# A bias table's way to its skewed form, and the place of one set of transposes, in a two-layer hybrid encoder

## The chip, the cores and the metric

The kernel runs on one core of one Trainium2 chip. Its time is the device time of one execution in microseconds (us). The core has five engines that run side by side and meet at semaphores: TensorE (PE: matmuls, and PEld, its weight loads), VectorE (DVE), ScalarE (ACT), GpSimd (POOL) and SyncE (SP), which here only issues DMA transfers. Transfers can be issued from SyncE's queue or from GpSimd's; both are carried out by the same 16 DMA engines.

## The reference, cut to what matters

Two layers work on 256 tokens of width 2048. Each layer reads RMSNorm(x) through one input projection, whose columns feed three mixers (gated linear attention, dilated windows with a relative bias, cross attention to a memory of 256 tokens), adds the output projection, then adds a squared-ReLU MLP of width 8192. All of it is float32.

```python
for l in range(DEPTH):
    h = rms_norm(x, norm_mix[l])
    proj = jnp.einsum('bsd,dk->bsk', h, w_in[l])
    (g_q, g_k, g_v, g_r, lr_f, lr_b, d_q, d_k, d_v, m_q) = split_columns(proj, IN_SPLITS)
    gla_out = gla_mixer(g_q, g_k, g_v, g_r, lr_f, lr_b, ...)
    dil_out = dilated_mixer(d_q, d_k, d_v, rel_bias, dil_norm[l])   # bias = rel_table[t5_bucket(j - i)]
    mem_out = memory_mixer(m_q, mem, mem_norm[l], w_mem_kv[l], mem_out_norm[l])
    mixed = jnp.concatenate([gla_out, dil_out, mem_out], axis=-1)
    x = x + jnp.einsum('bsk,kd->bsd', mixed, w_out[l])
    h = rms_norm(x, norm_mlp[l])
    u = jnp.square(jax.nn.relu(jnp.einsum('bsd,df->bsf', h, w_up[l])))
    x = x + jnp.einsum('bsf,fd->bsd', u, w_down[l])
```

## The kernel before

**Products.** Every float32 product is made of three matmuls on rounded halves: a weight quad (four blocks of 128 x 512, 1 MB, tile `raw`, three buffers) is loaded by `load_quad` (L189), ScalarE rounds it to `wh` (L203), VectorE makes the remainder `wl` (L204), each in two halves, and TensorE runs 24 matmuls per quad against the high and low halves of the activations (L221 to L223). `linear` does this for the four quads of one projection of 512 columns; `col(i)` is `linear` on the i-th such block of the input projection. `evac` (L231, ScalarE) scales a finished projection into a slot of a ring of 22 buffers that most of the kernel's middle tiles share.

**Order around the change.** The first layer starts with the memory: the keys' projection, then `bias_products`, then the values' projection, then `spread_bias`, then `col(9)` (the memory query mq), `col(0)` (the GLA query gq), `col(1)` (the GLA key gk), the memory attention, the gates, `col(2)` and `col(3)` (the GLA values), the GLA weights, and on to `col(6)`. The second layer runs in the same order without the bias. The activations of layer 0 come in transposed (`xT`, four pieces loaded by `split_loaded`, L173, the halves being x00h to x03h and x00l to x03l); `x` itself is loaded by GpSimd's queue (L569) once the squares of the memory have been taken from the same tile.

**The bias table.** `bias_products` makes, with one small matmul, `rows`: for each of 4 heads one row of 512 values by distance, in four partitions of on-chip memory. `spread_bias` (L259) writes each row 128 times into `scr`, a DRAM scratch of [4 heads, 128, 576]. `late_constants` (L275) reads `scr` back with a row step of 575, so that each partition gets its row shifted by one, as `bt` [128, 4, 384]. The dilated attention adds `bt` to its scores (L294).

**Transposes.** The operands of the attentions and of the GLA weights have to lie transposed. VectorE turns them in 16 blocks of 32 x 256 each (L108). These are generators in a work list, `turning`: `linear` takes one step (`turn(1)`) behind each quad's `wl`, and `issue_after` keeps the step's instructions behind that `wl`. km takes six steps (0, 4, 4, 4, 4 blocks, then the halves), mq four (0, 8, 8, then the halves), gq and gk six each (0, 4, 4, 4, 4, then the name is set). `turn()` without a number empties the list at once; `while "gkT" not in heads: turn(1)` ahead of the GLA weights takes the steps still missing, both without `issue_after`. The order of each engine's instructions is set when the kernel is built, by a planner with a model of the time; on the chip each engine works its list in order.

The lines and names that the steps below use: L173, L189, L203, L204, L221 to L223, L259, L275, L294, L569; tiles `raw`, `wh`, `wl`, `rows`, `scr`, `bt`, `gqT`, `gkT`, `gl` (the last tile of the gates, L391), `m_att`.

Of the kernel before, what the change touches and what calls it, by code (L numbers as in the profile page):

```python
# [11 lines left out]
F32 = mybir.dt.float32  # L12
# [8 lines left out]
P = 128  # L21
# [6 lines left out]
H = 4  # L28
# [9 lines left out]
NW = 512  # L38
# [4 lines left out]
def trunk_kernel(ctx: ExitStack, tc: tile.TileContext, a: dict):  # L43
    nc = tc.nc
# [7 lines left out]
    dram = ctx.enter_context(tc.tile_pool(name="scratch", bufs=1, space=DRAM))  # L52

    def slot(shape, name, dt=F32):
        return ring.tile([P] + shape, dt, tag="r", name=name)
# [15 lines left out]
    pending, turning = deque(), deque()  # L71

    def flush(n=None):
        for _ in range(len(pending) if n is None else min(n, len(pending))):
            pending.popleft()()
# [26 lines left out]
    def turn_blocks(o, v):  # L102

        src = v.rearrange("p t (b c) -> p t b c", b=4)
        dst = o.rearrange("p b (t s) -> p t b s", t=NT)
        for f in range(0, P, 32):
            for s in range(0, P, 32):
                yield nc.vector.transpose(  # L108
                    dst[f:f + 32, :, :, s:s + 32], src[s:s + 32, :, :, f:f + 32]
                )  # L110

    def paced(turns, steps):
        for n in steps:
            for _ in range(n):
                next(turns)
            yield
# [39 lines left out]
    def heads_turned(v, name, heads):  # L156

        o = slot([H, S], name)
        yield from paced(turn_blocks(o, v), (0, 4, 4, 4, 4))
        heads[name] = o  # L160

    def turn(n=None):

        while turning and n != 0:
            if next(turning[0], True):
                turning.popleft()
            n = n and n - 1
# [24 lines left out]
    def linear(wsrc, lhs, quads, loaded=(), pool=ps_mm, tag="mm"):  # L192

        ps = [pool.tile([P, NW], F32, tag=tag, name=f"mm{t}") for t in range(NT)]
        nq = len(quads)
        for i, q in enumerate(quads):
            raw, n = loaded[i] if i < len(loaded) else load_quad(wsrc, q)
            wh = [wpool.tile([P, 2, NW], F32R, tag="wh", name="wh", bufs=4) for _ in range(2)]
            wl = [wpool.tile([P, 2, NW], F32R, tag="wl", name="wl", bufs=4) for _ in range(2)]
            n = min(4 // n, 2)  # L200
            for k in range(0, 4, n):
                hi, lo = (w[k // 2][:, k % 2:k % 2 + n] for w in (wh, wl))
                nc.scalar.activation(hi, raw[:, k:k + n], AF.Copy)  # L203
                cut = nc.vector.tensor_tensor(lo, raw[:, k:k + n], hi.bitcast(F32), ALU.subtract)  # L204
            with tc.issue_after(cut.ins):
                turn(1)
            while q not in lhs:
                if pending:
                    flush(1)
                else:  # L210
                    turn(1)
            xh, xl = lhs[q]
            order = [(kk, t) for kk in range(4) for t in range(NT)]
            if i == nq - 1:
                order.sort(key=lambda o: o[1])
            for kk, t in order:
                sl = slice(t * P, (t + 1) * P)
                first = i == 0 and kk == 0
                last = i == nq - 1 and kk == 3
                hi, lo = wh[kk // 2][:, kk % 2, :], wl[kk // 2][:, kk % 2, :]  # L220
                nc.tensor.matmul(ps[t], xl[:, kk, sl], hi, start=first, stop=False)  # L221
                nc.tensor.matmul(ps[t], xh[:, kk, sl], lo, start=False, stop=False)  # L222
                nc.tensor.matmul(ps[t], xh[:, kk, sl], hi, start=False, stop=last)  # L223
            with tc.issue_after(cut.ins):
                flush(1)
        return ps

    def evac(ps, rs, name):
        o = slot([NT, NW], name)
        for t in range(NT):  # L230
            nc.scalar.activation(o[:, t, :], ps[t], AF.Copy, scale=rs[:, t:t + 1])  # L231
        return o
# [7 lines left out]
    def squares_of_x(norm, c):  # L240
        for t in range(NT):
            norm.add(c, t, xchunk(c, t))
# [2 lines left out]
    masks = const.tile([P, 2, H, P], U8, name="masks")  # L245
    tri = const.tile([P, 4, 320], F32R, name="tri")
    bt = const.tile([P, H, S + P], F32, name="bt")
    scr = dram.tile([H, P, SKEW], F32, name="scr")
    rel = work.tile([BUCKETS + 1, H], F32, name="rel", bufs=1)
    onehot = work.tile([P, NW], F32, tag="junk", name="onehot")[:BUCKETS + 1]  # L250
    rows = work.tile([P, NW], F32, tag="E", name="rows")[:H]

    def bias_products():
        ps = ps_mm.tile([P, NW], F32, tag="mm", name="biasps")[:H]
        nc.tensor.matmul(ps, rel, onehot, start=True, stop=True)
        nc.vector.tensor_copy(rows, ps)

    def spread_bias():
        nc.sync.dma_start(  # L259
            scr[:, :, :NW], rows.rearrange("h (o j) -> h o j", o=1).to_broadcast([H, P, NW])  # L260
        )

    def late_constants():
        tri32 = work.tile([P, 4, 320], F32, tag="E", name="tri32")
        nc.sync.dma_start(tri32, a["tri"])
        nc.vector.tensor_copy(tri, tri32)
        masks32 = slot([2, H, P], "masks32", mybir.dt.int32)
        nc.sync.dma_start(masks32, a["masks"])
        nc.vector.tensor_copy(masks, masks32)
        for h in range(H):  # L270
            v = bass.AP(
                tensor=scr.tensor, offset=scr.offset + h * P * SKEW + P - 1,
                ap=[[SKEW - 1, P], [1, S + P]],
            )
            nc.sync.dma_start(bt[:, h, :], v)  # L275

    def attend_weights(qT, kT, bias, name):

# [251 lines left out]
    def plan_loads(name, loads, src, gain, lhs):  # L530


        def step(i):
            for q in loads[i] if i < len(loads) else ():
                splits[name, q] = split_loaded(
                    slot([4, S], f"{name}{q}"), src, q, gain, f"{name}{q}", lhs
                )
                with tc.issue_after(newest[0]):
                    next(splits[name, q])
            if i:  # L540
                next(splits[name, i - 1], None)

        pending.extend([lambda i=i: step(i) for i in range(5)])

    up_groups = FF // FP // NW
    for l in range(DEPTH):
        w = a["w_in"]
        heads = {}
        col = lambda i: linear(w[l, i], xlhs, range(4))

        def keys_turned():
            turning.append(split_turned(km, "km", None, f"kmT{l}", heads, (0, 4, 4, 4, 4)))
# [6 lines left out]
        if l == 0:  # L559
            flush()  # L560
            bias_products()
            plan_loads("x0", ((0, 1), (2,), (3,)), a["xT"], gains[:, 0, 0, :], xlhs)
            ps_v = linear(a["w_mem"][l, 1], mem_lhs, range(4), pool=ps_ax, tag="ax")
            with tc.issue_after(newest[0]):
                spread_bias()

            def memory_squares(c):
                squares_of_x(mem_norm, c)
                nc.gpsimd.dma_start(x[:, :, c * NW:(c + 1) * NW], tokens(a["x"], c))  # L569

            pending.extend([lambda c=c: memory_squares(c) for c in range(4)])
            ps_q = col(9)
            flush()
            mem_rs = mem_norm.done()
            km = evac(ps_k, mem_rs, f"km{l}")
            vm = evac(ps_v, mem_rs, f"vm{l}")
            keys_turned()
            pending.extend([lambda c=c: squares_of_x(xnorm, c) for c in range(4)])
            ps_g = col(0)
            flush()  # L580
            rs = xnorm.done()
            nc.vector.tensor_scalar(rsq, rs, scale, None, ALU.mult)
            mq = evac(ps_q, rsq, "mq")
            queries_turned()
            gq = evac(ps_g, rsq, "gq")
            with tc.issue_after(newest[0]):
                late_constants()
        else:
            km = evac(ps_k, mem_rs, f"km{l}")
            keys_turned()  # L590
            vm = evac(linear(a["w_mem"][l, 1], mem_lhs, range(4)), mem_rs, f"vm{l}")
            ps_q = col(9)
            flush()
            rs = xnorm.done()
            nc.vector.tensor_scalar(rsq, rs, scale, None, ALU.mult)
            mq = evac(ps_q, rsq, "mq")
            queries_turned()
            gq = evac(col(0), rsq, "gq")
        ps_gk = col(1)
        turn()  # L600
        o_mem = attend_out(attend_weights(heads["mq"], heads["km"], None, "mem"), vm, "memo")
        turning.append(heads_turned(gq, "gqT", heads))
        gk = evac(ps_gk, rs, "gk")
        gates = log_gates(xlhs, rs, l)
        turning.append(heads_turned(gk, "gkT", heads))
# [43 lines left out]
        for part in range(FP):  # L649
# [22 lines left out]
            for g in range(4):  # L672
# [10 lines left out]
                if end and last and g < 3:  # L683
                    for t in range(NT):
                        v = xchunk(g, t)
# [4 lines left out]
    for t in range(NT):  # L690
        v = xchunk(3, t)
        fnorm.add(3, t, v)
        rs = fnorm.done(t)
        for half in (1, 0):
            for c in (2 * half, 2 * half + 1):
                v = xchunk(c, t)
# [107 lines left out]
```

## Time and profile before

| | us |
|---|---|
| three runs, median (lowest to highest) | 2277.84 (2275.19 to 2278.5) |
| the profiled execution, its own time | 2277.81 |
| its span, first to last instruction | 2276.0 |
| mean granted TensorE clock, share of full | 0.985 |
| TensorE busy | 2203.2 (97%) |
| VectorE busy | 1593.5 (70%) |
| ScalarE busy | 1133.8 (50%) |
| GpSimd busy | 38.2 (2%) |

All durations below come from that one profiled execution. Times are counted from the first instruction. An instruction's row gives its start, its duration and, in brackets, how long its engine stood idle before it and what ended that. Matmuls overlap, so a matmul's duration is longer than the distance to the next one's start; a stretch of matmuls is read by its first and last starts. The granted clock is a share of 2.4 GHz; 0.50 is 1.2 GHz.

### The profile page before, as it was taken

Reading aid. Unit: us, or ns where it says so; the run is one execution under the profiler, and the core shown is the slowest. Engines: PE = TensorE matmul, PEld = TensorE weight load, DVE = VectorE, ACT = ScalarE, POOL = GpSimd, SP = SyncE. Lnnn points to the kernel's source line nnn. Section 1 sums busy time; section 2 is a strip of 40 time slices with the busy share of each in tenths; the row PEclk is TensorE's granted clock in tenths of the full one; section 3 lists DMA queues with packets and bytes.
Section 4 is the critical chain, followed back from the end, with each engine's and each line's share of the span. In section 5 each row is a group of like instructions: output and inputs, shape, how many; then the busy total and the mean of one; then the engine's idle time right before and its main releaser. Section 6 shows DMA issues by size and latency. Waiting matters only on the chain.

```text
span 2276.0 us, 25766 instructions
## 1 busy us (share of the span) xinstructions
PE 2203.2 (97%) x9898; PEld 1822.8 (80%) x9898; DVE 1593.5 (70%) x2234; ACT 1133.8 (50%) x1529; POOL 38.2 (2%) x63
## 2 busy tenths in 40 slices
PE   7599999999999999999999989999999999999998
PEld 5487778888888888888888868888888888888886
DVE  5276787988558568567986487888864864765774
ACT  6256346555345345445654554655543543543543
POOL 1000000000000000000000000000000000000000
PEclk9799999999999999999999999999999999999999
DMA  8563435555555655555665533455555555555563
GB/s 296 151 222 127 151 130 175 192 189 195 194 198 185 203 188 192 195 188 201 218 207 188 181 115 127 166 186 203 185 199 190 191 197 196 193 193 196 187 220 129
DMA packets 63895, 423.26 MB, mean 186 GB/s; under 512 B 7035, under 2 KB 8315, under 8 KB 15004
## 3 DMA queue, kind: packets, MB, share of 16 engines
q1 hardware_dynamic: 63196, 419.53, 54.5%
q0 software_dynamic: 576, 2.10, 0.2%
q8 instruction: 77, 1.26, 0.2%
q14 instruction: 46, 0.38, 0.1%
HBM read 418.45 MB, written 3.15 MB: 185 GB/s over the span
## 4 chain that ended last, share of the span: by engine, by line
PE 92%; DVE 3%; DMA 3%; ACT 1%; issue 1%; SPq 0%; POOL 0%; ACTq 0%; POOLq 0%; DVEq 0%
PE mm L222 29%; PE mm L223 29%; PE mm L221 29%; DMA raw<-in_w_in 1%; DMA raw<-in_w_mem 1%; PE pv L322 1%; PE go L478 1%; DVE gqT L108 1%; DVE wl L204 1%; DVE gkT L108 1%; PE pT L308 0%; DVE dkT0o L108 0%; DMA x<-in_mem 0%; DVE dkT1o L108 0%; PE dg L438 0%
## 5 line engine op out<-in xcount | busy, mean ns | idle before, releaser
L204 DVE TENSOR_TENSOR wl<-raw,wh 128x1024 fp32r<-128x1024 f32 (+1 forms) x774 | 928.5, 1215 | 574.9 <-ACT wh L203 570.5
L203 ACT ACTIVATE wh<-raw 128x1024 fp32r<-128x1024 f32 (+1 forms) x774 | 813.9, 1053 | 893.1 <-PE mm L223 831.1
L222 PE MATMUL mm<-wl,uT3h 128*128 128x512 f32 x256 | 99.6, 389 | 0.0
L223 PE MATMUL mm<-wh,uT3h 128*128 128x512 f32 x256 | 99.6, 389 | 0.0
L221 PE MATMUL mm<-wh,zT0l 128*128 128x512 f32 x256 | 99.6, 389 | 0.0
L222 PE MATMUL mm<-wl,zT0h 128*128 128x512 f32 x256 | 99.6, 389 | 0.0
L223 PE MATMUL mm<-wh,zT0h 128*128 128x512 f32 x256 | 99.6, 389 | 0.0
L222 PE MATMUL mm<-wl,zT1h 128*128 128x512 f32 x256 | 99.6, 389 | 0.0
L223 PE MATMUL mm<-wh,zT1h 128*128 128x512 f32 x256 | 99.6, 389 | 0.0
L222 PE MATMUL mm<-wl,zT2h 128*128 128x512 f32 x256 | 99.6, 389 | 0.0
L223 PE MATMUL mm<-wh,zT2h 128*128 128x512 f32 x256 | 99.6, 389 | 0.0
L222 PE MATMUL mm<-wl,zT3h 128*128 128x512 f32 x256 | 99.6, 389 | 0.0
L223 PE MATMUL mm<-wh,zT3h 128*128 128x512 f32 x256 | 99.6, 389 | 0.0
L222 PE MATMUL mm<-wl,uT0h 128*128 128x512 f32 x256 | 99.6, 389 | 0.0
L223 PE MATMUL mm<-wh,uT0h 128*128 128x512 f32 x256 | 99.6, 389 | 0.0
L222 PE MATMUL mm<-wl,uT1h 128*128 128x512 f32 x256 | 99.6, 389 | 0.0
L223 PE MATMUL mm<-wh,uT1h 128*128 128x512 f32 x256 | 99.6, 389 | 0.0
L222 PE MATMUL mm<-wl,uT2h 128*128 128x512 f32 x256 | 99.6, 389 | 0.0
L223 PE MATMUL mm<-wh,uT2h 128*128 128x512 f32 x256 | 99.6, 389 | 0.0
L221 PE MATMUL mm<-wh,zT1l 128*128 128x512 f32 x256 | 99.4, 389 | 0.0
L221 PE MATMUL mm<-wh,uT1l 128*128 128x512 f32 x256 | 99.4, 389 | 0.0
L221 PE MATMUL mm<-wh,uT3l 128*128 128x512 f32 x256 | 99.3, 389 | 0.0
(435 smaller groups left out, 4682.8 us busy)
## 6 DMA issues: line engine op xcount, KB each, us to landing
raw<-in_w_up SPq DMA_DIRECT2D x128, 1024.0 KB, 4.9
raw<-in_w_down SPq DMA_DIRECT2D x128, 1024.0 KB, 4.9
raw<-in_w_in SPq DMA_DIRECT2D x80, 1024.0 KB, 4.9
raw<-in_w_out SPq DMA_DIRECT2D x32, 1024.0 KB, 4.9
raw<-in_w_mem SPq DMA_DIRECT2D x13, 1024.0 KB, 5.0
mem<-in_memT SPq DMA_DIRECT2D x7, 512.0 KB, 5.9
raw<-in_w_mem SPq DMA_DIRECT2D x12, 256.0 KB, 6.0
x<-in_mem SPq DMA_DIRECT2D x4, 512.0 KB, 6.9
```

Source lines behind the costliest of these rows:

```text
L108: yield nc.vector.transpose(dst[f:f + 32, :, :, s:s + 32], src[s:s + 32, :, :, f:f + 32])
L203: nc.scalar.activation(hi, raw[:, k:k + n], AF.Copy)
L204: cut = nc.vector.tensor_tensor(lo, raw[:, k:k + n], hi.bitcast(F32), ALU.subtract)
L221: nc.tensor.matmul(ps[t], xl[:, kk, sl], hi, start=first, stop=False)
L222: nc.tensor.matmul(ps[t], xh[:, kk, sl], lo, start=False, stop=False)
L223: nc.tensor.matmul(ps[t], xh[:, kk, sl], hi, start=False, stop=last)
L322: nc.tensor.matmul(ps[:, h, :], pT[s][:, h, t * P:(t + 1) * P], v[:, s, h * P:(h + 1) * P], start=s == 0, stop=s == NT - 1,)
L478: nc.tensor.matmul(ps[:, j, :], AT[s][:, t, 2 * c + j, :], v[c][:, s, j * DV:(j + 1) * DV], start=s == 0, stop=s == NT - 1,)
```

## The change

Two things change. The table now goes to DRAM once, into a new scratch `brow` [4, 512] (8 KB), and is spread from there into `scr` by a second transfer whose source repeats the 8 KB 128 times and whose destination is walked with the 128 rows outermost; both transfers, and the four loads of `bt`, are issued by GpSimd's queue instead of SyncE's. And gq's turns enter the work list before `col(1)` in place of after the memory attention; where the list was emptied after `col(1)`, steps are now taken only until mq is done. No arithmetic changes.

```diff
+    brow = dram.tile([H, NW], F32, name="brow")
     scr = dram.tile([H, P, SKEW], F32, name="scr")
...
     def spread_bias():
-        nc.sync.dma_start(
-            scr[:, :, :NW], rows.rearrange("h (o j) -> h o j", o=1).to_broadcast([H, P, NW])
-        )
+        nc.gpsimd.dma_start(brow, rows)
+        src = bass.AP(tensor=brow.tensor, offset=brow.offset, ap=[[0, P], [NW, H], [1, NW]])
+        nc.gpsimd.dma_start(scr[:, :, :NW].rearrange("h p j -> p h j"), src)
...
-            nc.sync.dma_start(bt[:, h, :], v)
+            nc.gpsimd.dma_start(bt[:, h, :], v)
...
             gq = evac(col(0), rsq, "gq")
+        turning.append(heads_turned(gq, "gqT", heads))
         ps_gk = col(1)
-        turn()
+        while "mq" not in heads:
+            turn(1)
         o_mem = attend_out(attend_weights(heads["mq"], heads["km"], None, "mem"), vm, "memo")
-        turning.append(heads_turned(gq, "gqT", heads))
```

## Rows read from the trace of the kernel before

**Rows 1.** The page's 40 slices: TensorE's busy tenths.

```profile
PE   7599999999999999999999989999999999999998
```

**Rows 2.** TensorE's waits: total us, times, longest us.

```profile
PE mm L221 <- ACT wh L203: 35.7, 5, 27.3
PE mm L222 <- DVE wl L204: 25.6, 7, 9.7
```

**Rows 3.** Timeline, 35 to 100 us: start, us, engine, line, idle before.

```profile
35.55 0.78 SPq L259 DMA_DIRECT2D scr<-rows  x1
36.37 21.43 SPq L173 DMA_DIRECT2D x<-in_xT  x1
57.91 11.46 SPq L189 DMA_DIRECT2D raw<-in_w_in  x3
...
87.53 1.70 ACT L127 ACTIVATE x03h<-x,gains 128x256 fp32r<-128x256 f32 x4 [31.56 <-DMA x<-in_xT]
91.19 1.22 PE L221 MATMUL mm<-wh,x00l 128*128 128x512 f32 x2 [27.26 <-ACT wh L203]
99.56 0.62 PE L221 MATMUL mm<-wh,x01l 128*128 128x512 f32 x2
```

**Rows 4.** Windows: stretch, length, busy us by engine, granted clock, DMA share, GB/s.

```profile
40.00:44.00 4.00, 1.92 (x8) 0.95 (x6) 0.84 (x1) 1.93 (x3) 0.00 (x0) 1.00 1.04 431
46.00:58.00 12.00, 10.84 (x41) 8.20 (x40) 7.39 (x13) 9.96 (x24) 0.90 (x2) 0.88 0.25 34
76.00:86.00 10.00, 0.00 (x0) 0.00 (x0) 0.00 (x0) 0.00 (x0) 0.00 (x0) 0.50 0.24 36
```

**Rows 5.** DMA issues: queue, count, KB each, median us to landing.

```profile
x<-in_x POOLq DMA_DIRECT2D x4, 512.0 KB, 10.2
scr<-rows SPq DMA_DIRECT2D x1, 1024.0 KB
```

**Rows 6.** Timeline: first matmuls of two quads in a row at full clock.

```profile
115.88 0.39 PE L221 MATMUL mm<-wh,x00l 128*128 128x512 f32 x1
...
121.32 0.39 PE L221 MATMUL mm<-wh,x01l 128*128 128x512 f32 x1
```

**Rows 7.** Timeline, layer 1 before the GLA weights: VectorE, then TensorE.

```profile
1324.00 1.22 DVE L391 TENSOR_TENSOR gl<-z,gh 128x1024 fp32r<-128x1024 f32 x1
1325.13 7.18 DVE L108 STREAM_TRANSPOSE gqT<-gq 32x256 f32<-32x256 f32 x16
1332.34 7.20 DVE L108 STREAM_TRANSPOSE gkT<-gk 32x256 f32<-32x256 f32 x16
...
1340.18 3.49 DVE L204 TENSOR_TENSOR wl<-raw,wh 128x1024 fp32r<-128x1024 f32 x3
...
1341.45 0.80 PE L222 MATMUL mm<-wl,xT0h 128*128 128x512 f32 x1 [9.67 <-DVE wl L204]
...
1345.89 0.66 PE L221 MATMUL mm<-wh,xT1l 128*128 128x512 f32 x2
```

**Rows 8.** Timeline: the same turns in layer 0.

```profile
216.05 7.18 DVE L108 STREAM_TRANSPOSE gqT<-gq 32x256 f32<-32x256 f32 x16
```

**Rows 9.** DMA packets, 15 to 20 us, then 181.5 to 183.5 us (gbias).

```profile
DMA packets 906, 1.86 MB, mean 371 GB/s; under 512 B 128, under 2 KB 128, under 8 KB 906
DMA packets 173, 0.58 MB, mean 288 GB/s; under 512 B 25, under 2 KB 25, under 8 KB 170
```

**Rows 10.** Timeline: GpSimd.

```profile
28.49 0.72 POOL L569 DMA_DIRECT2D x<-in_x  x1 [0.50 <-ACT junk L93]
...
50.86 0.19 POOL L79 TENSOR_SCALAR m_mix<-ss_mix 128x2 f32<-128x2 f32 x1 [18.73 <-DVE ss_mix L99]
...
179.46 0.19 POOL L79 TENSOR_SCALAR m_att<-ssh 128x4 f32<-128x4 f32 x1 [127.62 <-ACT junk L329]
```

**Rows 11.** The tile bt: its readers, first and last start.

```profile
L294 DVE TENSOR_TENSOR dilp<-sc,bt x8: 681/683/692, 337.0 to 1455.1; 128x512 f32<-128x512 f32 x8
```

**Rows 12.** Window of layer 1's col(1): columns as in rows 4.

```profile
1246.50:1268.50 22.00, 22.00 (x99) 18.22 (x98) 9.91 (x9) 9.17 (x10) 0.00 (x0) 1.00 0.58 197
```

## The prediction

> **What bounds the kernel now.** First the page: in its 40 slices TensorE is full but for the first three, one in the middle and the last [rows 1]. So time can be won only where TensorE waits. The next view is therefore the list of waits, TensorE's own rows [rows 2]: over the whole span it waited 35.7 us for wh (ScalarE's rounding of a weight quad), 27.3 of it in one piece, and 25.6 us for wl (VectorE's remainder), the longest piece 9.7 us. Two places hold most of that.
>
> The first is at 64 us. In the timeline TensorE stands still for 27.26 us before 91.19 [rows 3]. It waits for wh of the first quad of the projection `col(9)`; ScalarE, in order, is stuck ahead of that on x03h, 31.56 us, because the last piece of xT has not landed. Above it SyncE's queue shows why: `scr<-rows` is issued at 35.55, the issue of x<-in_xT behind it takes 21.43 us, and the w_in loads come only at 57.91. The windows show what the DMA engines did meanwhile [rows 4]: full (1.04) up to 44 us, then 0.25 of 16 engines from 46 to 58 and 0.24 from 76 to 86, at 34 and 36 GB/s. That is four engines carrying the bias broadcast of 1024 KB [rows 5]: at some 25 to 36 GB/s it needs 30 to 41 us, from about 44 to 85, and the loads that share those four engines' queue end after it. When TensorE resumes, its granted clock in 76 to 86 had been 0.50 (1.2 GHz): the 24 matmuls from 91.19 to 99.56 [rows 3] took 8.37 us against 5.44 us for the same 24 from 115.88 to 121.32 [rows 6]. That is another 2.93 us.
>
> The second place stands once in each layer, before the GLA weights. In layer 1 VectorE ends the gate work (gl) at 1325.2, turns gq in 7.18 us, gk in 7.20 us, and only then makes the wl for which TensorE has been idle 9.67 us, until 1341.45 [rows 7]. The next ten matmuls (1341.45 to 1345.89) take 4.44 us instead of 10/24 of 5.44 = 2.27: 2.2 us of low clock. Layer 0 has the same block of turns at 216.05 [rows 8].
>
> **The bias table: what goes.** The broadcast leaves SyncE's queue and no longer reads four SBUF partitions; the destination is walked with 128 rows outermost instead of four heads. xT's last piece then issues at about 35.6. The w_in quads issue when a raw buffer frees (three of them): the first three at about 45, 54 and 58 us, not at 57.91 and after. From 46 us the engines are nearly free [rows 4]. So x03h, then wh and wl of the first quad, are due by some 62 us, ahead of TensorE's end of the memory projection at 63.93 (91.19 less 27.26). Gain: 27.26 + 2.93 = 30.2 us. What is late next: the second quad's wl, due 69.4 (63.93 + 5.44), ready by about 68, since vm is evacuated before it. That is the thinnest cover; a miss costs 1 to 3 us.
>
> **What comes.** An 8 KB store of `rows` on GpSimd's queue, a wait for it, then 512 rows of 2 KB from DRAM to DRAM, 32 for each of 16 engines. No row of before shows a DRAM to DRAM copy; the bounds: in a stretch of mostly 2 KB loads at a full DMA share 906 packets took 5 us, 16 x 5/906 = 88 ns each [rows 9], so 32 x 88 ns = 2.8 us; at the other end it keeps the old rate, 41 us. A hot source is the question, as one 8 KB block is read 128 times. The nearest row is the load of gbias, which is also one row read 128 times: 173 packets, 0.58 MB in 2 us at 288 GB/s [rows 9], against 371 GB/s. I take 3 to 6 us. Its place: the four x loads of GpSimd's queue, the last issued at 28.49 [rows 10], lie in front of it and take 10.2 us to land [rows 5], so the store lands near 41 and the broadcast runs near 43 to 49, where the engines were idle. Any overlap with the saturated time before 44 delays the w_mem quads by at most the 3 us that the copy needs; I charge 1 us, range 0 to 3.
>
> What the four GpSimd waits hold up: behind the store's wait stand the mixing norm's two small instructions (from 50.86, used for mq, which in the new order comes at 63.93 + 4 x 5.44 = 85.7); behind the four bt loads, which wait for the broadcast, nothing until m_att, at 179.46 before [rows 10]. bt is first read at 337 us [rows 11]. I charge nothing; if the broadcast lasted past 86 us this cover would be gone, and TensorE would wait for it one for one.
>
> A rule of the skill meets a row here. The share of 0.24 says four engines, 25 GB/s or a little more in all. The Trainium skill ("DMA: Bandwidth & Descriptors", Why a DMA increments its semaphore by 16) has the engine count set by the outermost dimension, here 4, then 16; the trace agrees for the 4. If engines alone were the limit, the new copy would go at four times the old rate, about 10 us, and the sum would not change.
>
> **The GLA query: what moves.** Only the order of the work list changes. In layer 0 km and mq still fill all four turns of `col(1)`, and the loop that replaces `turn()` stops when mq is done: gq is reached at the same place as before, and the 9.7 us there stay. In layer 1 km and mq are done before `col(1)`, so gq's first 12 of 16 blocks run there and the last four in the next projection. Cover: from 1246.5 to 1268.5 TensorE was full and VectorE busy only 9.91 of 22 us [rows 12]; 12 x 0.45 = 5.4 us fit. Uncovered, they would cost those 5.4 us. Then gk's turns follow gl directly, and wl comes 7.2 us earlier: 1334.3. TensorE, out of work at 1331.78 (1341.45 less 9.67), would idle 2.5 us. I leave gk's turns where they are: its tile is allocated in program order after the last gl, as gqT was. The low clock of 2.2 us should shrink; an idle of about 2 us in 40 to 44 (TensorE busy 1.92 of 4) was followed by a clock of 0.88 in 46 to 58 [rows 4], so I keep 1.1 us of it. Gain: 7.2 + 1.1 = 8.3 us, range 5.4 (7.2 less 1.8 if one four-block piece stays in the way) to 11.9 (the whole idle and its low clock).
>
> **Sum.** 30.2 - 1.0 + 8.3 = 37.5 us off 2277.81, the profiled execution's own time (span 2276.0 and 1.8 around it), which lies at the median of the runs, 2277.84. Forecast 2240.3 us; its own range 2235 (nothing charged, and the whole idle of layer 1 gone: 30.2 + 11.9 = 42.1) to 2246 (3 us of overlap, 3 for the second quad, 5.4 for layer 1 and about 3 for a plan that orders other work differently).
>
> **Rivals.**
> - The query's turns bring nothing, because VectorE's queue still puts them behind gl: 2240.3 + 8.3 = 2248.6. For it: gq lay ready since its evacuation and waited all the same in both layers; against: in the new order its tile comes before the attention's tiles.
> - The first projection stalls anew, on ScalarE's order or on late loads: 10 us back, 2250. For it: ScalarE and VectorE share every step from 42 to 60; against: the engines idle from 46.
> - A hot source at the old total rate. 32 packets on each engine would take 41 us, 1.3 us each; alternating with 8 KB weight packets (0.30 us each at the full rate of [rows 4], 16 x 8 KB at 431 GB/s) a quad of 8 packets per engine loads in 8 x 1.6 = 13 us until 85. xT's piece, 8 packets of half that size, would land at about 56, the quads at 69, 82 and 88; with some 3 us of rounding behind each, they would start at 72, 85 and 91 instead of 63.9, 69.4 and 74.8: 16 us back, 2256. Against it: gbias.
> - **Slower than before**: the same mechanism further down. TensorE's wait for wh in `col(9)` passes the 37.5 us saved once the broadcast lasts past some 107 us, 63 us long, 17 GB/s; at 10 GB/s (105 us) all loads creep until 149, some 80 us back, 2320. The Trainium skill ("SBUF — State Buffer", A bandwidth-pool intuition that's wrong) puts one HBM port at about 22.5 GB/s; by that an 8 KB block behind one port would copy in an estimated 47 us, near the case before this one. The gbias row, 288 GB/s, speaks against it.
> - The change doesn't do what it says for the table: the broadcast still runs on four engines in front of the loads, only the query's 8.3 us come: 2269.5.
>
> **How the numbers follow.** Forecast 0.68, query without effect 0.12, new stall 0.09, hot source 0.06, slower 0.03, four engines 0.02. The range leaves out the last three and the low tail: 2235 to 2251. A measurement of this kernel tells about 0.2% (4.6 us) from no change. All cases but one are faster by more; with a little for the unforeseen: faster 0.95, within 0.2% 0.01, slower 0.04.
>
> **What would show it.** TensorE's row at the first x00 quad near 64 without a long wait; x<-in_xT issued in under 1 us; the DMA share between 44 and 50 above 0.25 on GpSimd's queue; gqT's first 12 turns of layer 1 inside `col(1)`, some 75 us ahead of gl's end and VectorE's block before the GLA weights 7.2 us long; layer 0's 9.7 us unchanged. Wrong would be: a DMA share that stays near 1 with low GB/s after 50, or gqT's turns still behind gl in layer 1.

## The result, and the profile after

| | before | changed |
|---|---|---|
| median (lowest to highest), us | 2276.52 (2274.6 to 2278.5) | 2235.47 (2233.11 to 2237.74) |
| ratio, 95% interval | | 0.982 [0.9803, 0.9837] |
| profiled execution: time, span | 2277.81, 2276.0 | 2234.38, 2232.6 |
| mean granted clock | 0.985 | 0.996 |

The change takes 41.05 us by the medians and 43.43 us between the two profiled executions. The forecast was 2240.3, with a range of 2235 to 2251. The sign and both places were right, the query's mechanism too, and of the reason given for the table one half; the gain was 3.6 us larger than forecast by the medians and 5.9 us by the profiled executions, and the time lies at the lower edge of the range.

Line numbers of the changed kernel are one to three higher than before behind the edit (L391 is L392, L275 is L276). First the slices of its page, which answer [rows 1]: the hole in the second and third slice is gone.

```profile
PE   7998999999999999999999999999999999999998
```

TensorE's waits (us in all, times, longest), which answer [rows 2]. Of the wait for wh the 27.3 us piece is gone and 5.5 at the very start is now the longest; the wait for wl has lost one of its two 9.7 us pieces.

```profile
PE mm L222 <- DVE wl L204: 16.3, 6, 9.7
PE mm L221 <- ACT wh L203: 11.0, 4, 5.5
```

The timeline of the start, which answers [rows 3] (start, duration, engine, line, idle before): GpSimd's issues, then SyncE's, then the first matmul of the first two quads of `col(9)`.

```profile
25.12 0.56 POOL L260 DMA_DIRECT2D brow<-rows  x1
...
34.80 0.85 POOL L262 DMA_DIRECT2D scr<-brow  x1 [5.96 <-DMA brow<-rows]
49.99 0.19 POOL L79 TENSOR_SCALAR m_mix<-ss_mix 128x2 f32<-128x2 f32 x1 [14.35 <-DVE ss_mix L99]
...
50.95 2.23 POOL L276 DMA_DIRECT2D bt<-scr  x4
...
35.70 0.60 SPq L173 DMA_DIRECT2D x<-in_xT  x1
44.67 24.43 SPq L189 DMA_DIRECT2D raw<-in_w_in  x5
...
64.51 0.61 PE L221 MATMUL mm<-wh,x00l 128*128 128x512 f32 x2
...
69.95 0.61 PE L221 MATMUL mm<-wh,x01l 128*128 128x512 f32 x2
```

The last piece of xT is issued in 0.60 us where it took 21.43; the w_in loads begin at 44.67 where they began at 57.91; TensorE goes from the memory projection into `col(9)` with no wait, and the 24 matmuls to the next quad take 5.44 us, full clock, where they took 8.37. The windows (stretch, length, busy us by engine, granted clock, DMA share, GB/s) answer [rows 4]:

```profile
40.00:44.00 4.00, 2.26 (x9) 1.25 (x8) 1.72 (x2) 2.81 (x5) 0.00 (x0) 1.00 1.04 430
44.00:46.00 2.00, 2.00 (x11) 1.60 (x9) 2.00 (x5) 2.00 (x7) 0.00 (x0) 1.00 1.03 426
46.00:50.00 4.00, 2.88 (x13) 2.06 (x11) 0.39 (x2) 4.00 (x14) 0.01 (x1) 1.00 1.01 419
50.00:58.00 8.00, 6.36 (x20) 4.83 (x21) 6.98 (x11) 7.64 (x13) 3.10 (x6) 0.79 0.89 306
```

A share near 1 now means bytes: 419 to 430 GB/s up to 50 us, where four engines had carried 34. The spread copy is part of it; it needs 13.5 us from issue to landing (from the view of the issues below, which answers [rows 5]), since it shares the engines with the weight loads; a run below has it on free engines in 6.5 us.

```profile
scr<-brow POOLq DMA_DIRECT2D x1, 1024.0 KB, 13.5
```

The second place, layer 1 before the GLA weights, answers [rows 7]: gq's turns stand far ahead in four pieces (first and last shown), gk's follow the last gate step (gl) directly, and wl follows gk's.

```profile
1218.23 1.77 DVE L108 STREAM_TRANSPOSE gqT<-gq 32x256 f32<-32x256 f32 x4
...
1234.09 1.80 DVE L108 STREAM_TRANSPOSE gqT<-gq 32x256 f32<-32x256 f32 x4
...
1292.51 1.22 DVE L392 TENSOR_TENSOR gl<-z,gh 128x1024 fp32r<-128x1024 f32 x1
1293.65 7.18 DVE L108 STREAM_TRANSPOSE gkT<-gk 32x256 f32<-32x256 f32 x16
...
1300.86 3.50 DVE L204 TENSOR_TENSOR wl<-raw,wh 128x1024 fp32r<-128x1024 f32 x3
...
1302.14 0.50 PE L222 MATMUL mm<-wl,xT0h 128*128 128x512 f32 x1 [1.84 <-DVE wl L204]
...
1304.58 0.62 PE L221 MATMUL mm<-wh,xT1l 128*128 128x512 f32 x2
```

Layer 0 has, as [rows 8] had, both sets of turns in one block behind gl, and its wait:

```profile
186.44 7.18 DVE L108 STREAM_TRANSPOSE gqT<-gq 32x256 f32<-32x256 f32 x16
193.65 7.20 DVE L108 STREAM_TRANSPOSE gkT<-gk 32x256 f32<-32x256 f32 x16
...
202.76 0.80 PE L222 MATMUL mm<-wl,x00h 128*128 128x512 f32 x1 [9.68 <-DVE wl L204]
```

**Where the 43 us come from.** The start of the same quad in both traces gives the lead of the changed kernel at that point; the steps in it are the gains (those under 0.3 us are left out).

| place (start before, start after) | lead, us | step, us |
|---|---|---|
| first quad of `col(9)` (91.19, 64.51) | 26.68 | 26.68 |
| second quad (99.56, 69.95) | 29.61 | 2.93 |
| layer 0, behind the GLA wait | 30.1 | 0.5 |
| layer 0, quad at 297.67 after | 31.49 | 1.37 |
| layer 1, behind the GLA wait (1345.89, 1304.58) | 41.31 | 9.83 |
| layer 1, quad at 1392.60 after | 43.18 | 1.82 |
| last matmul (2266.02, 2222.83) | 43.19 | |

### The profile page after: what moved, and what is told of

Same layout as the page of the kernel before. It is cut to its first block, busy times and chain, and to the rows that moved or that the text cites. A ratio compares the mean times of both kernels' runs of the same rounds, so it can differ in the third digit from the quotient of the medians.

```text
span 2232.6 us, 25769 instructions
## 1 busy us (share of the span) xinstructions
PE 2195.7 (98%) x9898; PEld 1818.4 (81%) x9898; DVE 1593.3 (71%) x2234; ACT 1133.5 (51%) x1529; POOL 39.7 (2%) x69
## 4 chain that ended last, share of the span: by engine, by line
PE 94%; DVE 2%; DMA 2%; ACT 1%; issue 1%; SPq 0%; POOL 0%; ACTq 0%; POOLq 0%; DVEq 0%
PE mm L222 30%; PE mm L223 30%; PE mm L221 30%; DMA raw<-in_w_mem 1%; PE pv L323 1%; PE go L479 1%; DVE gkT L108 1%; DVE wl L204 0%; PE pT L309 0%; DVE gqT L108 0%; DMA x<-in_mem 0%; DVE dkT0o L108 0%; PE dg L439 0%; ACT junk L93 0%; PE dg L443 0%
```

## Experiments

All runs are compared with the kernel before on the same chip. The two parts of the change were first taken apart.

**The table alone** (the changed kernel with the work list of before):

```diff
-        turning.append(heads_turned(gq, "gqT", heads))
         ps_gk = col(1)
-        while "mq" not in heads:
-            turn(1)
+        turn()
...
+        turning.append(heads_turned(gq, "gqT", heads))
```

> The changed kernel with the query's turns put back behind the memory attention; only the bias table's new way is left. If the two parts are separate, as the account by matmul starts says (29.6 us ahead after the first projection, some 2 us of clock and small stalls in layer 0): 30 to 32 us below the kernel before, some 2245, with TensorE's 27.26 us wait gone and the 9.7 us wait of layer 1 back. If the early loads also serve layer 1 (the rival): over 36 us below.

Measured: 2247.31 us (2245.24 to 2248.9), ratio 0.9871 [0.9856, 0.9886], 29.9 less than 2277.22 before. TensorE's list of waits has the 25.6 us for wl back, and not the long one for wh:

```profile
PE mm L222 <- DVE wl L204: 25.6, 7, 9.7
PE mm L221 <- ACT wh L203: 10.2, 4, 5.4
```

**The query alone** (the kernel before with the new place of gq's turns; the diff is the last one reversed, on the old table):

> The kernel before with the query's turns moved and nothing else. Separate parts: 9 to 12 us below the kernel before (7.8 us of idle, 2 us of low clock, up to 1.8 us of a later stall), some 2266, with the 27.26 us wait at 64 us unchanged. Rival, that the query's turns only serve once the table is out of the way: within 3 us of the kernel before.

Measured: 2265.14 us (2262.76 to 2266.08), ratio 0.9948 [0.9934, 0.9963], 12.1 less than before. The long wait of the start remains:

```profile
90.56 1.22 PE L221 MATMUL mm<-wh,x00l 128*128 128x512 f32 x2 [25.00 <-ACT wh L203]
```

29.9 and 12.1 make 42.0, against 41.05 for both: within the spread of the runs the two parts add up. The query's lead has the same two steps in layer 1 as in the whole change, 9.87 and 1.82.

**What about the table was it?** The change moves the copy to GpSimd's queue, takes its source from DRAM, and walks its destination in another order. The prediction counted all of this as one step. Two runs take them apart. First the old copy, from on-chip memory, issued by GpSimd:

```diff
-        nc.gpsimd.dma_start(brow, rows)
-        src = bass.AP(tensor=brow.tensor, offset=brow.offset, ap=[[0, P], [NW, H], [1, NW]])
-        nc.gpsimd.dma_start(scr[:, :, :NW].rearrange("h p j -> p h j"), src)
+        nc.gpsimd.dma_start(
+            scr[:, :, :NW], rows.rearrange("h (o j) -> h o j", o=1).to_broadcast([H, P, NW])
+        )
```

> The changed kernel, but the broadcast is the old one (512 rows straight from four partitions, heads outermost), only issued by GpSimd's queue. Theory, that the loss was the loads standing behind the broadcast in one queue: the copy still crawls for some 40 us at 25 GB/s on four engines, yet the loads take turns with it there, 8 packets of a quad in 8 x (0.31 + 0.31) = 5.0 us, under the 5.44 us that TensorE needs for a quad; within 4 us of the changed kernel (2234 to 2240). Rival, that the slow copy itself must go: TensorE's wait at 64 us comes back by 10 us or more, 2246 and up.

Measured: 2265.8 us (2264.85 to 2266.3), ratio 0.9952 [0.9938, 0.9967]. That is the query's 12 us and nothing of the table's 30: what I expected here was wrong. The timeline and a window show the same stall in another place:

```profile
24.97 1.15 POOL L259 DMA_DIRECT2D scr<-rows  x1 [0.22 <-issue]
26.11 1.45 POOL L569 DMA_DIRECT2D x<-in_x  x2
...
76.36 2.23 POOL L275 DMA_DIRECT2D bt<-scr  x4 [47.66 <-DMA scr<-rows]
...
77.41 0.63 ACT L93 ACTIVATE junk<-x 128x512 f32<-128x512 f32 x1 [28.10 <-DMA x<-in_x]
...
81.05 1.22 PE L221 MATMUL mm<-wh,mem02l 128*128 128x512 f32 x2 [28.96 <-ACT wh L203]
```

```profile
64.00:76.00 12.00, 0.00 (x0) 0.00 (x0) 0.00 (x0) 0.00 (x0) 0.00 (x0) 0.50 0.25 54
```

The copy holds a quarter of the engines as before. Behind it in GpSimd's queue now lie the last two loads of x (26.11), ScalarE stands for 28.10 us in front of the squares of x (junk), and the wh of a memory quad is stuck behind those. Another queue only chose another victim.

Then the new copy, with its store and the bt loads, issued by SyncE, the queue of before (`nc.gpsimd.dma_start` to `nc.sync.dma_start` in those three places):

> The changed kernel with all its table transfers issued by SyncE: store, wait for it, spread from DRAM, four loads of bt. Theory, that the copy's source and walk are what counts: the store lands near 46 us, behind the loads already queued, and holds xT's last piece and the first w_in quad until then; they land by about 53, x03h is due by 55, so at most 3 us are lost against the changed kernel, 2235 to 2239. Rival, that an in-order wait on SyncE must be kept off its queue: 5 to 15 us lost, 2240 to 2250.

Measured: 2234.16 us (2233.05 to 2235.84), ratio 0.9816 [0.98, 0.9833], the changed kernel's time and a little under the 2235 to 2239 that I had expected. Issued later, when the engines are free, the spread lands in 6.5 us (timeline, issues, and the packets from 48 to 52 us):

```profile
47.43 0.65 SPq L262 DMA_DIRECT2D scr<-brow  x1
...
scr<-brow SPq DMA_DIRECT2D x1, 1024.0 KB, 6.5
...
DMA packets 534, 1.52 MB, mean 379 GB/s; under 512 B 24, under 2 KB 24, under 8 KB 458
```

So the queue is worth nothing, and all of the 30 us belongs to the copy's source and walk. A source block of 8 KB read 128 times costs nothing visible: 379 GB/s in a stretch that holds the copy and some weight loads. No run has the DRAM source with the four heads outermost, so what the walk does for that source was not measured by itself.

**Source or number of engines?** The old copy named four heads outermost and ran on four engines. Here it is issued as four transfers from on-chip memory, one head each, so that the outermost dimension is 128:

```diff
+        for h in range(H):
+            nc.sync.dma_start(
+                scr[h:h + 1, :, :NW],
+                rows[h:h + 1, :].rearrange("h (o j) -> h o j", o=1).to_broadcast([1, P, NW]),
+            )
```

> The changed kernel's query part; the table goes straight from on-chip memory into scr again, but as four transfers of one head each (one partition of rows repeated 128 times, 256 KB), issued by SyncE, with the bt loads on SyncE too. The old copy named four heads outermost and kept a quarter of the DMA engines busy (share 0.24 to 0.25 at 34 to 57 GB/s in the kernel before and in the old copy on GpSimd's queue). If the number of engines was the limit, each of these four transfers spreads over all of them, the copy takes about 10 us at a share near 1, and the start-up wait is gone: 2234 to 2245 us. If reading so few partitions was the limit, the four transfers take as long in all as the old one (about 41 us at 25 GB/s), now at a share near 1 with low GB/s, and the wait of 25 to 29 us ahead of the first x00 quad is back: 2262 to 2270 us, or more if the loads behind it on the same engines are late as well.

Measured: 2262.31 us (2261.39 to 2264.09), ratio 0.9934 [0.9918, 0.9951]. The windows show all engines taken and the old rate, and TensorE's row the old wait:

```profile
50.00:58.00 8.00, 6.49 (x21) 4.94 (x22) 7.12 (x12) 4.97 (x8) 0.77 (x2) 0.79 0.91 27
58.00:64.00 6.00, 6.00 (x28) 4.99 (x27) 0.76 (x2) 0.00 (x0) 0.00 (x0) 1.00 0.91 27
```

```profile
86.45 1.22 PE L221 MATMUL mm<-wh,x00l 128*128 128x512 f32 x2 [22.02 <-ACT wh L203]
```

A share of 0.91 at 27 GB/s: all sixteen engines are taken, and the copy is no faster. The number of engines was not the limit. The landings, recorded for the first and the last of the four transfers, show how they ran (KB each, us to landing; issues from 35 to 36 us, then from 37 to 38 us, where the third transfer is counted too):

```profile
scr<-rows SPq DMA_DIRECT2D x1, 256.0 KB, 19.6
```

```profile
scr<-rows SPq DMA_DIRECT2D x2, 256.0 KB, 44.2
```

Issued at 35.4 and 37.3, they landed at 55.0 and 81.5 us. So the heads went one behind the other, in some 9 us each, and one partition alone gave 27 GB/s, as much as four had given together in the old copy (1024 KB from about 44 to 85 us, 25 to 26 GB/s). That already speaks against a limit of 6 to 7 GB/s for each partition, which the next two runs were still built on.

**How many partitions?** The matmul that makes `rows` can be given each head's column several times; the rows then lie in more partitions and the copy repeats each less often. One transfer on SyncE again, 64 partitions repeated 8 times, and 16 repeated 32 times (R is 16 and 4):

```diff
+        nc.vector.tensor_copy(relr, rel.rearrange("b (h o) -> b h o", o=1).to_broadcast([BUCKETS + 1, H, R]))
+        nc.tensor.matmul(ps, relr.rearrange("b h r -> b (h r)"), onehot, start=True, stop=True)
...
+        nc.sync.dma_start(
+            scr[:, :, :NW].rearrange("h (r k) j -> (h r) k j", r=R),
+            rows.rearrange("p (o j) -> p o j", o=1).to_broadcast([R * H, P // R, NW]),
+        )
```

> The changed kernel's query part; the table goes straight from on-chip memory into scr by one transfer on SyncE, but the matmul that makes rows is given each head's column 16 times, so that the four rows lie in 64 partitions, each repeated 8 times by the copy instead of 128 times. The two copies from four partitions came to 25 to 27 GB/s in all, on four engines and on all of them. Theory: the limit is the reading of one partition, some 6 to 7 GB/s each; with 64 partitions the copy runs at the rate of any other transfer, is done in 3 to 6 us, and the time is the changed kernel's, 2232 to 2238 us. Rival: on-chip memory as the source of repeated rows is the limit, however many partitions hold them; then 25 GB/s and a start-up wait of 22 to 29 us again, 2260 to 2268 us.

> The same with each head's column given 4 times: 16 partitions, each repeated 32 times. By the theory of the single partition the copy moves at four times 25 to 27 GB/s, about 100 GB/s, and takes 10 us; it is done near 56 us, before TensorE runs out of quads at 64 us, so the wait is mostly gone: 2233 to 2244 us. By the rival it is 2260 to 2268 us as before.

Measured: 2236.36 us (2234.91 to 2238.55), ratio 0.9824 [0.9807, 0.9842], with 64; 2236.58 us (2233.09 to 2237.67), ratio 0.9819 [0.9804, 0.9835], with 16. Both are the changed kernel's time, without the way through DRAM. The packets while the copy had the engines nearly to itself: 64 partitions from 46 to 48 us, then 16 partitions from 47 to 50 us.

```profile
DMA packets 352, 0.76 MB, mean 378 GB/s; under 512 B 5, under 2 KB 5, under 8 KB 346
```

```profile
DMA packets 162, 0.33 MB, mean 110 GB/s; under 512 B 1, under 2 KB 1, under 8 KB 162
```

27, 110 and 378 GB/s for 4, 16 and 64 partitions: the rate goes with the partitions until the engines are full (the 378 holds a few weight packets). On-chip memory is not a slow source as such.

**Each partition, or each group of neighbours?** Four transfers of one head each again, but read from partitions 0, 4, 8 and 12 (`rows` made as for the 16 partitions):

```diff
-                rows[h:h + 1, :].rearrange("h (o j) -> h o j", o=1).to_broadcast([1, P, NW]),
+                rows[4 * h:4 * h + 1, :].rearrange("h (o j) -> h o j", o=1).to_broadcast([1, P, NW]),
```

> As the run head by head: four transfers of one head each on SyncE, 128 repeats of one partition's row, but the four rows are read from partitions 0, 4, 8 and 12 in place of 0, 1, 2 and 3 (the matmul that makes rows is given each head's column 4 times, and the first of each four is read). Four neighbouring partitions gave 25 to 27 GB/s in all, 16 neighbouring ones about 104. If each partition has 6 to 7 GB/s for itself, four partitions again give 25 to 27 GB/s however far apart, the copy lasts from 46 to 76 us and the time is that of the run head by head, 2258 to 2266 us. If neighbouring groups of four share one way out of on-chip memory, the four rows now have four ways, together about 100 GB/s; the copy takes some 10 us and the time is that of the 16 partitions, 2233 to 2244 us. The Trainium skill (SBUF - State Buffer, Door 1: The DMA port swizzle) puts four neighbouring partitions on one port of about 27 GB/s and speaks for the second.

Measured: 2240.42 us (2239.11 to 2243.39), ratio 0.9846 [0.983, 0.9863]: 22 us less than with four neighbours. The issues of that run and of the one with neighbours (KB each, median us to landing, of the first and the last transfer):

```profile
scr<-rows SPq DMA_DIRECT2D x4, 256.0 KB, 19.7
```

```profile
scr<-rows SPq DMA_DIRECT2D x4, 256.0 KB, 31.9
```

So four neighbouring partitions share one way of about 27 GB/s, and partitions four apart have ways of their own. The first x00 quad starts without a wait. I had expected about 100 GB/s; 46 to 52 us show 81, 84 and 153 GB/s with some weight loads in them. The heads still come one behind the other in the queue, so that the four ways would overlap only in part; that is an argument, and no run shows it.

**The query's place.** In the prediction gk's turns stay behind gl, and layer 0's gq turns too, because their tiles are allocated in program order after the gates. Whether this is the reason was tried by writing the first four blocks of the turns ahead of the gates: gk's in both layers, gq's in layer 0, and both. The step that does it also allocates the tile, so allocation and first write move together here and are not told apart.

```diff
         while "mq" not in heads:
             turn(1)
+        if l == 0:
+            turn(2)
...
+        gk_turns = heads_turned(gk, "gkT", heads)
+        next(gk_turns), next(gk_turns)
         gates = log_gates(xlhs, rs, l)
-        turning.append(heads_turned(gk, "gkT", heads))
+        turning.append(gk_turns)
```

> The changed kernel with the first four blocks of gk's turns written ahead of the gates in both layers, so that its ring slot is taken there. Theory: what keeps turns behind the last gate step is the place of a tile's first write in the order of the program (ring slots go round in that order), not the work list. Then gkT's other 12 blocks fall in between the quads as gqT's do in layer 1 of the changed kernel, layer 1 loses its remaining wait of 1.84 us ahead of the GLA weights, and in layer 0 only gq's 7.2 us stay behind the gates, so the 9.68 us wait falls to about 2.5 us: 7.2 + 1.8 = 9 us less, with up to 2 us of low clock on top, 2223 to 2227 us where the changed kernel gives 2235. Rival: the turns are held by the work list's pace or by VectorE's load alone; then they stay a block of 16 behind the gates and the time stays within 2 us of the changed kernel's.

> The changed kernel with, in layer 0 alone, two more steps of the work list taken ahead of the memory attention, which writes gq's first four blocks there. By the theory of the first write, layer 0's gq turns leave the gates' end and its 9.68 us wait falls by 7.2 us, with up to 2 us of low clock on top; layer 1 is the changed kernel's: 2226 to 2229 us. By the rival (the pace of the work list, not the first write), gq's 16 blocks stay behind the gates and the time is the changed kernel's, 2233 to 2237 us.

> The last two edits together on the changed kernel: no turn is left behind the gates in either layer. Theory: layer 0's wait of 9.68 us and layer 1's of 1.84 us both go, with 0 to 2 us of low clock: 2235.5 - 11.5 = 2224 us, 2221 to 2225. If the two single edits each take the whole of layer 0's wait down to what the other leaves, the sum is less than theirs added, since the wait can't fall below zero. Rival: the turns set in between the earlier quads delay those quads' remainders, and new waits of the same total appear ahead of the quads of the key and the values; then it stays at 2230 us or above.

Measured, against 2277.78 us before:

| | us | ratio |
|---|---|---|
| gk | 2227.31 (2226.13 to 2228.03) | 0.9779 [0.9764, 0.9794] |
| gq in layer 0 | 2225.9 (2224.84 to 2227.19) | 0.9774 [0.9759, 0.9788] |
| both | 2221.5 (2219.38 to 2222.74) | 0.9753 [0.9738, 0.9768] |

They lie 8.2, 9.6 and 14.0 us below the changed kernel's 2235.47. Both together is inside the range that the theory of the first write gave; the two single edits miss theirs by 0.3 us above (gk) and 0.1 us below (gq), and all are far from the rivals' times. With both, TensorE's waits for wl fall from 16.3 to 3.5 us, the longest from 9.7 to 1.5; in layer 1 the last four of gk's turns stand 30 us ahead of gl, and wl follows gl directly:

```profile
PE mm L222 <- DVE wl L204: 3.5, 5, 1.5
```

```profile
1253.41 1.80 DVE L108 STREAM_TRANSPOSE gkT<-gk 32x256 f32<-32x256 f32 x4
...
1283.11 1.23 DVE L392 TENSOR_TENSOR gl<-z,gh 128x1024 fp32r<-128x1024 f32 x1
1284.26 2.35 DVE L204 TENSOR_TENSOR wl<-raw,wh 128x1024 fp32r<-128x1024 f32 x2
```

The version with both is faster than the kernel before and than the changed kernel (0.6% by the medians of their runs; their intervals against before don't overlap).

## Why the prediction was right, point by point

- **What bounds, and where.** Right. The two waits that the prediction took from [rows 2] are the two that paid.
- **The table, 30.2 us less 1.0.** Right in size: 26.68 and 2.93 make 29.61 against 29.2. The charge of 1.0 for overlap can't be read from the runs: the first x00 quad starts at 64.51, 0.6 us after the memory projection's end in the kernel before (63.93), but the five kernels that are the same up to there (the changed one, the table alone, the three early writes) have it anywhere from 62.52 to 64.51. The 26.68 has the same uncertainty. The thinnest cover, the second quad's wl, held: no wait at 69.95.
- **The reason given for it.** Right in part. "The broadcast leaves SyncE's queue" stands first in the step, and it is worth nothing: the old copy on GpSimd's queue kept the stall, the new copy on SyncE's queue has none. "No longer reads four SBUF partitions" is the part that carries it. The walk with 128 rows outermost brings all engines in (share 0.91 head by head) and did nothing for the slow source; what it is worth with the DRAM source was not tried by itself.
- **The Trainium skill's rule on engines.** The Trainium skill ("DMA: Bandwidth & Descriptors", Why a DMA increments its semaphore by 16) sets the number of engines by the outermost dimension, and the shares agree: 0.25 with 4 outermost, 0.91 with 128. By engines alone the new copy was to take an estimated 10 us; head by head, on all engines, its last quarter landed at 81.5 us, 44.2 us after its issue, and the copy from DRAM took 6.5. So the rule holds for the count and does not price this copy.
- **The new copy's cost.** "3 to 6 us" holds on free engines (6.5 from issue to landing). Its place was wrong: the store was put among the x loads (25.12), not behind them, so the copy ran from 34.80 in the saturated time and took 13.5 us. No cost of it stands out of the 2 us by which the start varies.
- **The rivals.** A hot source and a slower copy both fell: 379 GB/s in a stretch that holds the spread. By the figure that the Trainium skill ("SBUF — State Buffer", A bandwidth-pool intuition that's wrong) gives for one HBM port, 22.5 GB/s, it would have taken an estimated 47 us; the 6.5 us measured show no such limit. The query without effect and the new stall fell too: gqT's turns begin 75 us ahead of gl's end in layer 1, and `col(9)` starts without a wait.
- **GpSimd's queue, nothing charged.** Right for what the change does: bt is issued at 50.95 behind m_mix, and m_att has no wait for it. The run with the old copy shows what the cover was worth: the x loads in the same queue cost 28.10 us once they lay behind a slow copy.
- **The query, 8.3 us.** Mechanism right, size too small. Of the layer 1 step of 9.83 us, 7.83 are idle time (9.67 to 1.84), where 7.2 were forecast: before, `qd` (0.69 us, at 1339.57) also stood between the turns and wl, and now it stands behind wl (1306.07). The rest is the low clock, of which the prediction kept 1.1 of 2.2 us and which vanished whole: the ten matmuls from 1302.14 to 1304.58 take 2.44 us where they took 4.44. A further 1.82 us comes from a later wait of 1.50 us for wl at 1430.38 before, which the table alone keeps (1.48 us) and the query alone takes away. Before, one half of wl (1424.37) stands ahead of a block of eight dkT1o turns (1425.51 to 1429.07) and three behind it; in the changed kernel and with the query alone two halves stand ahead of that block (1379.87). The prediction did not look that far down VectorE's list.
- **Layer 0 unchanged.** Right for its 9.68 us. The 1.87 us that the changed kernel gained there is no part of the change that I can name; 1.37 of it is the clock, below, and the other 0.5 lies behind the 9.68 us wait, where the granted clock of the next 5 us was 0.57 before and 0.68 after.
- **The upper end.** The forecast's own range ends at 2246, but its terms (3, 3, 5.4 and about 3), added up, give 2251, which is where the range as stated ends.

The failing term is thus the query's, 8.3 against 9.83 and 1.82; with the 1.87 of layer 0 and 0.4 at the start it makes 5.6 of the 5.9 us between the 37.5 forecast and the 43.43 of the profiled executions.

## What to carry to other kernels

A transfer that repeats a few rows out of on-chip memory goes at a rate set by how many groups of four neighbouring partitions it reads at a time, here whatever its queue and the number of engines; make the rows in 16 or more partitions, which here cost one small copy ahead of a matmul that was there anyway, or send them through DRAM once. A slow transfer stalls whatever lies behind it on its engines, so look at share and GB/s together: 0.25 at 34 and 0.91 at 27 were the same fault. And where tiles come from a ring in program order, a late block of work may be late only for the place of its first write: four blocks written early let the other twelve follow.

## What the runs showed of the hardware

**The rate out of few partitions.** 27 GB/s from four neighbouring partitions, however many engines ask, and as much from one alone; 110 from 16, 378 from 64. The Trainium skill ("SBUF — State Buffer", Door 1: The DMA port swizzle) puts four neighbours on one port and gives 27.6 and 104 GB/s for partitions 0 to 3 and 0 to 15; the runs agree, and I had not applied it to a source. The same table of the Trainium skill gives 196 GB/s for partitions 0 to 63; the 378 GB/s here disagree, and the measurement decides: 341 of the 352 packets are between 2 and 8 KB, where the weight loads have larger ones, and as 2 KB rows they alone make an estimated 350 GB/s.

**The same wait, with and without a lower clock.** In layer 0 there is a wait of 2.74 us for wl in both kernels. Windows of 5 us behind it, before and then after:

```profile
322.40:327.40 5.00, 4.99 (x17) 4.07 (x18) 5.00 (x6) 1.02 (x1) 0.00 (x0) 0.70 0.55 197
```

```profile
292.30:297.30 5.00, 5.00 (x23) 4.17 (x24) 5.00 (x6) 1.06 (x1) 0.00 (x0) 1.00 0.61 202
```

The granted clock is 0.70 in the one and 1.00 in the other, 1.37 us apart. The table alone, the query alone and the 16 partitions show 0.66 to 0.71 behind the same wait, the new copy on SyncE and the 64 partitions 1.00. So a wait of this length sometimes brings the lower level (1.2 GHz) and sometimes not, and a kernel's time moves by over 1 us with it. Behind 9.7 us it fell in the windows looked at (0.50 before in layer 1, 0.59 after in layer 0), behind 1.84 us it stayed at 1.00.
